# Hybrid decoder trunk on one core: forget-gate tile cleared first, a planner whose operations overlap, and first halves' sums of squares that add two k tiles on VectorE

## The chip, the core and the metric

One core of one Trainium2 chip runs the whole program. The metric is the device time of one execution in microseconds. It is taken as the median of several runs: 1278.13 us for the kernel before, of three runs between 1277.13 and 1283.45. The engines that matter are TensorE (PE, with its weight loads PEld), VectorE (DVE), ScalarE (ACT), GpSimd (POOL) and SyncE (SP), which only issues transfers.

## The reference

Two layers of a decoder trunk work on one sequence of 512 tokens, with 16 learned meta tokens in front (528 rows, width 1024, float32). A layer has a mixer and a feed-forward part (FFN), each between two RMS norms:

```python
h = h + rms_norm(mixer(rms_norm(h, pre_g)), post_g)
h = h + rms_norm(ffn(rms_norm(h, pre_g)), post_g)

def rms_norm(x, g):
    return x * rsqrt(mean(x * x, axis=-1) + 1e-6) * g
```

The mixer makes one projection `w_in` of the normed rows. Its columns are q, k and v of eight attention heads, eight forget-gate logits, a gated convolution of 31 taps and a short one of 3 taps. The attention's logits carry a running sum of the forget gates' logarithms:

```python
log_f = log_sigmoid(f_logit + b_forget)
F = cumsum(log_f, axis=1)
s = q @ k.T * scale + F[:, :, None] - F[:, None, :]    # causal
y_attn = softmax(s) @ v
```

The three groups are normed by head, concatenated and projected by `w_out`. The FFN (inner width 2816) projects up to a gate and a value, passes both through a convolution of 3 taps, and projects `silu(gate) * value` down.

## The kernel before

**Layout.** Activations lie transposed: 128 features in the partitions, 528 rows along the free axis, so the width of 1024 is 8 k tiles (`KD`). Rows are worked in two halves of 264, which the code calls `hf` 0 and 1. Every product in float32 is made from a high and a low part of each operand, `uhi`, `ulo`, `whi`, `wlo`, `yhi`, `ylo`: three matmuls for each product, high by high, high by low and low by high (`mm3`, whose matmuls have L668, and `First.steps`, L709). ACT casts the high part (a weight's at L608, with L2049 for the FFN's up weights and their sums), and DVE takes the low part as the difference. The FFN's up projection combines blocks of weights and of activations so that seven products (L2198) do the work of eight; POOL issues transfers that add weights onto weights for it (`raw<-u`, `u<-raw`, L2086), and their results `s1` to `s4` are split on ACT and DVE as well. A product's result is copied out of PSUM by ACT (`z` at L2211, `yp` at L2373).

**Who sets the order.** The kernel doesn't issue its work in program order. Class `Flow` is a planner: `act`, `dve`, `gp` and `flow.op` hand in operations with an engine, an estimated duration, what they wait for and a priority, and generators hand in stretches of matmuls. `Flow.run` keeps a clock for each engine (`self.free`) and one for TensorE (`self.pe`), always takes what can start first, and moves that engine's clock by the estimated duration. The order in which it takes operations is the order in which they stand in each engine's queue. An engine works its queue strictly in order: where one operation waits, all behind it wait. Where the plan has TensorE idle for longer than `flow.least` (2.0 us, in the mixer 0.7), `Flow.run` puts in idle matmuls of a constant, the fillers (L1775, 128x128).

**Norms.** The sum of squares over the 1024 features of a half goes through class `Norms`. For each pair of k tiles ACT squares 128 x 2 x 264 values (L749; at times DVE does), and DVE adds them onto `acc`, a tile with two slices, one for each k tile of the pair (L765). The last pairs can stay apart as tiles `c` of their own (`n_apart`). `factor` then sums over the partitions: for each of these parts, two matmuls with the constant `om_d` (L792), one for each slice, all into one PSUM tile. These are plain float32. From that ACT and DVE work out the factor (L805 to L812) with which the half is scaled. A norm has a key: ("y", hf) is the norm behind a sub-layer, ("h", hf) the one ahead of the next.

**The mixer's start.** Convolution taps run on DVE (L937, L987, L989). At the same time POOL clears tiles for the attention: parts of `vhi`, `vlo`, `vals`, of `k` and `q` tiles and of `dm` (L439 is the helper `mset`), then `fx` (L1151). `fx` takes the forget-gate logits: `v_proj` makes v in five blocks of rows (L1204), and for each block ACT copies `vhi`, DVE makes `vlo` (L1181) and DVE adds the bias to the eight logit columns into `fx` (L1184). The PSUM bank is free again after these. `forget_gate` then takes logarithm and running sum: DVE prepares `fpre` (L1239), TensorE sums (L1244), DVE copies to `gt` (L1245), TensorE transposes (L1253).

**The attention.** Its matmuls are the logits (L1361, L1405), products of probabilities `ph`, `pl` and v (L1462), and column terms from `dm` (L1385). The remaining projection matmuls (L668) and the convolution's work are planned in between.

## Time and profile before

| | |
|---|---|
| median of three runs | 1278.13 us (1277.13 to 1283.45) |
| the profiled execution | 1277.56 us |
| its span | 1275.8 us |
| mean granted clock of TensorE | 0.995 |
| TensorE busy | 1239.5 us, 97% |
| VectorE busy | 967.7 us, 76% |
| ScalarE busy | 775.6 us, 61% |
| GpSimd busy | 236.2 us, 19% |
| fillers, records of L1775 | 58 |
| VectorE's wait for fx, both layers | 13.1 us |

The span runs from the first to the last instruction that the profiler saw; the execution's own time is 1.8 us longer. A row of the timeline gives the start, the busy time, the engine, the line, the operation, its output and inputs, their shape and how many were put together; in brackets stands the idle time ahead of it and what ended it. A row of the chain of waits gives start, length and the piece of work. A row of a group gives busy time and mean nanoseconds of one. A window's row gives its bounds and length, then for PE, PEld, DVE, ACT and POOL the busy time and the number of instructions, then the clock granted, the DMA share and GB/s. The plain float32 matmuls of `om_d` are recorded twice each.

### The profile page before, as it was taken

The page shows a single profiled execution, that of the slowest core. Times are in us where ns is not written, and L with a number is a line of the kernel's source. Part 1 is how long each engine was busy: PE and PEld are TensorE (multiplying, and loading weights), DVE is VectorE, ACT ScalarE, POOL GpSimd, SP SyncE. Part 2 cuts the span into 40 slices and gives each one's busy share as a digit, 9 for nine tenths or more (in the row PEclk, how much of TensorE's full clock was granted, in tenths as well). Part 3 has the DMA queues.
Part 4 walks back from the last instruction along what each step waited for, and adds up shares of the span by engine and source line. Part 5 has one row for each costly group of instructions (what it writes and reads, how often), then busy time and mean ns, then how long its engine had stood idle before and what let it go on. Part 6 is the DMA issues. An engine that isn't in the chain of part 4 may idle for free.

```text
span 1275.8 us, 24511 instructions
## 1 busy us (share of the span) xinstructions
PE 1239.5 (97%) x9468; PEld 1188.3 (93%) x9468; DVE 967.7 (76%) x1752; ACT 775.6 (61%) x1571; POOL 236.2 (19%) x415
## 2 busy tenths in 40 slices
PE   9999999999999999999999999999998999999996
PEld 8988988999999999999999899889997999999986
DVE  7598877588866777788676988766887587778865
ACT  7256668667755555556672666785676565556552
POOL 1314320002122222120003233200022122122200
PEclk9999999999999999999999999999999999999998
DMA  7131131636486866776340322216386677768641
GB/s 225 51 102 52 47 113 34 206 119 167 102 195 139 188 156 154 172 161 183 115 140 18 111 76 68 60 58 213 131 175 136 155 160 169 163 148 185 144 141 66
DMA packets 73942, 165.85 MB, mean 130 GB/s; under 512 B 8081, under 2 KB 26641, under 8 KB 73313
## 3 DMA queue, kind: packets, MB, share of 16 engines
q1 hardware_dynamic: 52048, 124.86, 30.6%
q0 software_dynamic: 21360, 39.02, 19.0%
q8 instruction: 74, 1.21, 0.4%
q10 hardware_dynamic: 416, 0.40, 0.1%
q14 instruction: 44, 0.35, 0.1%
HBM read 129.14 MB, written 8.65 MB: 108 GB/s over the span
## 4 chain that ended last, share of the span: by engine, by line
PE 79%; DVE 8%; ACT 4%; issue 4%; DMA 2%; POOL 2%; DVEq 0%; ACTq 0%; POOLq 0%
PE psum L668 37%; PE psum L2198 25%; PE psum L709 6%; PE psum L1462 2%; PE psum L1204 2%; PE psum L792 2%; PE psum L1405 1%; DVE cacc L937 1%; DMA c<-acc 1%; DMA raw<-in_w_dram 1%; PE psum L1361 1%; POOL q L439 1%; DMA raw<-u 1%; POOL k L439 1%; PE psum L1532 1%
## 5 line engine op out<-in xcount | busy, mean ns | idle before, releaser
L668 PE MATMUL psum<-yhi,whi 128*128 128x264 f32 (+3 forms) x660 | 187.9, 299 | 3.6 <-ACT yp L2373 2.1
L668 PE MATMUL psum<-ylo,whi 128*128 128x264 f32 (+3 forms) x660 | 184.7, 295 | 1.1 <-DVE ylo L2175 0.8
L668 PE MATMUL psum<-yhi,wlo 128*128 128x264 f32 (+3 forms) x660 | 184.3, 294 | 0.2 <-DVE wlo L612 0.2
L668 PE MATMUL psum<-uhi,whi 128*128 128x264 f32 (+1 forms) x640 | 165.2, 291 | 1.2 <-DVE q L1292 1.2
L668 PE MATMUL psum<-ulo,whi 128*128 128x264 f32 (+1 forms) x640 | 161.0, 284 | 0.5 <-DVE ulo L1947 0.5
L668 PE MATMUL psum<-uhi,wlo 128*128 128x264 f32 (+1 forms) x640 | 160.7, 284 | 0.0
L2124 DVE SCALAR_TENSOR_TENSOR c<-z,pv,c 128x528 f32<-128x528 f32 (+1 forms) x156 | 117.1, 757 | 29.0 <-ACT c L2122 26.4
L612 DVE TENSOR_TENSOR wlo<-raw,whi 128x1024 fp32r<-128x1024 f32 (+2 forms) x84 | 100.5, 1205 | 38.1 <-ACT whi L608 37.1
L668 PEld LDWEIGHTS psum<-yhi,whi 128*128 128x128 f32 x660 | 120.3, 188 | 9.1 <-ACT yp L2373 2.5
L668 PEld LDWEIGHTS psum<-ylo,whi 128*128 128x128 f32 x660 | 120.4, 188 | 4.4 <-DVE ylo L1088 1.1
L668 PEld LDWEIGHTS psum<-yhi,wlo 128*128 128x128 f32 x660 | 120.4, 189 | 3.2 <-DVE wlo L612 0.6
L668 PEld LDWEIGHTS psum<-uhi,whi 128*128 128x128 f32 x640 | 111.9, 188 | 4.4 <-issue 2.4
L2211 ACT COPY z<-psum 128x264 f32<-128x264 f32 (+2 forms) x128 | 48.2, 377 | 107.2 <-PE psum L2198 106.5
L668 PEld LDWEIGHTS psum<-ulo,whi 128*128 128x128 f32 x640 | 112.2, 188 | 0.9 <-DVE ulo L1947 0.7
L668 PEld LDWEIGHTS psum<-uhi,wlo 128*128 128x128 f32 x640 | 112.1, 188 | 0.4 <-DVE wlo L612 0.4
L608 ACT CAST whi<-raw 128x1024 fp32r<-128x1024 f32 (+2 forms) x84 | 85.8, 1034 | 38.7 <-DMA raw<-in_w_dram 20.4
L937 DVE SCALAR_TENSOR_TENSOR cacc<-apad,pv,cacc 128x528 f32<-128x528 f32 x120 | 88.6, 766 | 0.3
L709 PE MATMUL psum<-uhi,whi 128*128 128x264 f32 (+1 forms) x320 | 85.0, 289 | 1.3 <-ACT uhi L840 1.3
L709 PE MATMUL psum<-uhi,wlo 128*128 128x264 f32 (+1 forms) x320 | 83.4, 283 | 0.0
L2052 DVE TENSOR_TENSOR wlo<-raw,whi 128x1024 fp32r<-128x1024 f32 (+4 forms) x78 | 76.4, 980 | 8.6 <-ACT whi L2049 8.2
L2049 ACT CAST whi<-raw 128x1024 fp32r<-128x1024 f32 (+4 forms) x78 | 66.3, 855 | 15.5 <-PE psum L668 10.3
L2198 PE MATMUL psum<-uhi,whi 128*128 128x264 f32 (+1 forms) x256 | 72.8, 284 | 2.2 <-ACT yp L2373 2.2
(317 smaller groups left out, 3732.4 us busy)
## 6 DMA issues: line engine op xcount, KB each, us to landing
raw<-in_w_dram SPq DMA_DIRECT2D x110, 512.0 KB
u<-in_w_dram SPq DMA_DIRECT2D x32, 512.0 KB
u<-in_w_dram POOLq DMA_DIRECT2D x32, 256.0 KB, 5.3
raw<-in_w_dram POOLq DMA_DIRECT2D x32, 256.0 KB, 4.1
u<-raw POOLq DMA_DIRECT2D x32, 256.0 KB, 4.0
raw<-u POOLq DMA_DIRECT2D x32, 256.0 KB, 4.2
raw<-in_w_dram SPq DMA_DIRECT2D x16, 448.0 KB
h_mid<-h SPq DMA_DIRECT2D x4, 1056.0 KB
```

The source lines that it names most:

```text
L439: nc.gpsimd.memset(t.bitcast(F32), val)
L608: nc.scalar.copy(box["hi"][:, :sz], box["raw"][:, :sz])
L612: nc.vector.tensor_sub(lo[:, :sz], box["raw"][:, :sz], box["hi"][:, :sz].bitcast(F32))
L668: nc.tensor.matmul(d, lhsT=w[a][:, k, cols], rhs=rhs(b, k, hf), start=start and i == 0 and p == 0, stop=stop and i == n - 1 and p == 2)
L709: nc.tensor.matmul(self.ps[hf, i], lhsT=self.ws[i].w[a][:, k, :], rhs=self.rhs(b, k, hf), start=k + a + b == 0, stop=k == KD - 1 and b == 1)
L792: nc.tensor.matmul(ps, lhsT=om_d, rhs=box["c"][:, i, :], start=j + i == 0, stop=j + 1 == n_parts and i == 1)
L937: nc.vector.scalar_tensor_tensor(conv[j], in0=src, in1=conv[j], scalar=col("a_dw_w", CK * j + i), op0=ALU.mult, op1=ALU.add)
L2049: nc.scalar.copy(box[name][0], raw())
L2052: return a, dve(dve_us(n), lambda: nc.vector.tensor_sub(box[name][1], raw(), box[name][0].bitcast(F32)), a, prio=prio)
L2124: nc.vector.scalar_tensor_tensor(c, in0=z[:, i:i + n], scalar=wtap(i, t), in1=c, op0=ALU.mult, op1=ALU.add)
L2198: nc.tensor.matmul(d, lhsT=w[i][:, P * k:P * (k + 1)], rhs=terms[b][j][k](), start=start and k + p == 0, stop=k == KH - 1 and p == 2, skip ...
L2211: done[f, name] = act(us, lambda: nc.scalar.copy(z_of(f, e)[:, zin[h]], d[:, lo:]), *after, prio=0)
```

## The change

Three things change. The first is the place at which `fx` is made and cleared: it is now the first tile of the attention's pool, ahead of `vhi`, and its memset is the first of POOL's block.

The second is in the planner. An operation on DVE now gives its engine free 0.08 us before the estimated end, one on ACT 0.095 us before it; when its result is there is counted as before. No instruction is added or taken away by that, but the order of all engines is planned anew.

The third is in the norms. For keys in `norms.folds`, once `acc` is complete, DVE adds its second slice onto its first (128 x 264), and TensorE makes one matmul with `om_d` on the first slice where it made two. That is so for one norm at the opening (("h", 1)), for ("y", 0) and ("h", 0) behind each mixer and behind the first layer's FFN, and for ("y", 0) behind the last FFN: eight in all. VectorE has eight operations more. TensorE has eight matmuls with `om_d` fewer in the norms and 14 fillers fewer (29 to 15). `HOP_US` and `ADD_LAT` only give numbers a name.

```diff
--- before.py
+++ after.py
@@ -56,6 +56,10 @@
 WE = 0.5
 YS = (9, 9)
 NWARM = 10
+PFOLD = 0
+FOLD = ((("h", 1),), (("y", 0), ("h", 0)), (("y", 0), ("h", 0)))
+HOP_US = 0.06
+OVER = {"dve": 0.08, "act": 0.095}
 K1 = 2
 SQD = (2, 6)
 FILLED = 0.8
@@ -69,7 +73,8 @@
 FILL_US = 0.225
 OH = {(0, 0): -3, (0, 4): -2.9, (0, 6): -2.8, **{(1, k): -0.4 for k in range(0, KD, 2)}}
 OW = (-0.46, -0.459)
-ADD_US, ADD_LAT = 1.2, 3.6
+ADD_US = 1.2
+ADD_LAT = 3.6
 PT = ((0.8035, 0.8055), (0.8035, 0.8055))
 D0 = ((0, 0, 0, 0, 5, 10, 15, 20), (0, 0, 0, 0, 5, 10, 15, 20))
 
@@ -249,7 +254,7 @@
 
 
 
-    HOP = 0.06
+    HOP = HOP_US
 
     def __init__(self):
         self.pe = 0.0
@@ -337,7 +342,7 @@
                 for r, slot in takes:
                     r.take(slot)
                 fn()
-                self.free[eng] = start + us
+                self.free[eng] = start + us - OVER.get(eng, 0.0)
                 tok.time = start + us + lat
                 continue
             if self.rings and start > self.pe:
@@ -720,7 +725,7 @@
 
 
         def __init__(self, pool, rs, nc=4, **apart):
-            self.pool, self.nc = pool, nc
+            self.pool, self.nc, self.folds = pool, nc, ()
             self.c, self.acc = Ring(nc), Ring(2)
             self.factors(rs, **apart)
 
@@ -768,6 +773,12 @@
             if k == 0 or k >= KD - 2 * apart:
                 s["parts"][max(0, k // 2 - KD // 2 + apart + 1) if k else 0] = box, slot
                 box["at"] = [a]
+            if k == KD - 2 * apart - 2 and key in self.folds:
+                def fold():
+                    t = s["acc"]["c"]
+                    nc.vector.tensor_add(t[:, 0, :], t[:, 0, :], t[:, 1, :])
+
+                s["at"] = dve(dve_us(n), fold, s["at"], prio=prio + PFOLD)
             if k == KD - 2 * apart - 2:
                 s["acc"]["at"], s["acc"]["there"] = [s["at"]], True
             return a
@@ -788,9 +799,10 @@
                     ps = psum[:, p_slot.buf, :n]
                 s = self.sums[key]
                 box, slot = s["parts"][j]
-                for i in range(2):
-                    nc.tensor.matmul(ps, lhsT=om_d, rhs=box["c"][:, i, :], start=j + i == 0, stop=j + 1 == n_parts and i == 1)
-                tok = flow.mm(2 * 0.0017 * n)
+                m = 1 if j == 0 and key in self.folds else 2
+                for i in range(m):
+                    nc.tensor.matmul(ps, lhsT=om_d, rhs=box["c"][:, i, :], start=j + i == 0, stop=j + 1 == n_parts and i + 1 == m)
+                tok = flow.mm(m * 0.0017 * n)
                 slot.close(tok)
             s["free"] = mine = Slot()
             us, vs = act_us(n), dve_us(n)
@@ -1110,6 +1122,8 @@
         sc_done = {}
 
 
+        fx = T(ap, [P, 5, HEADS], F32, "fx")
+        nc.gpsimd.memset(fx, 0.0)
         vhi = T(ap, [P, 5, WHOLE, VW], F32R, "vhi")
         vlo = T(ap, [P, 5, WHOLE, VW], F32R, "vlo")
         pw_place[0] = lambda: T(ap, [P, 5, WHOLE, VW], F32R, "vlo").rearrange("p b h d -> p (b h d)")
@@ -1147,8 +1161,6 @@
             dm = T(ap, [P, L], F32R, f"dm{j}")
             mset(dm[:, :N_META], 0.0)
             dms.append(dm)
-        fx = T(ap, [P, 5, HEADS], F32, "fx")
-        nc.gpsimd.memset(fx, 0.0)
         gt = T(ap, [P, 5, HEADS], F32, "gt")
         g_hl = [T(mp, [P, L], F32, "sq", 2)[:HEADS].bitcast(F32R) for _ in range(2)]
 
@@ -1793,6 +1805,7 @@
         plan_w(after_mixer[0])
         norms = Norms(sp, [T(sp, [P, L], F32, f"rs{i}", 1) for i in range(NRS)], NCS, h=APS)
         norms.apart["h", 0] = KD // 2 - 1
+        norms.folds = FOLD[0]
         hg, hg_at = T(sp, [P, KD, L], F32, "hg", 1), {}
         for hf in range(2):
             for k in range(0, KD, 2):
@@ -1861,6 +1874,7 @@
             first = First(u_in, iws, {})
             rs = T(fp, [P, L], F32, "rs", 1)
             norms = Norms(fp, [rs])
+            norms.folds = FOLD[1]
             plan = ExitStack()
             plan.enter_context(tc.manual_schedule(engines=every))
             flow.yields = YF[l]
@@ -2473,6 +2487,7 @@
                 wpos[0] += 2
                 rs, rz = (T(fp, [P, L], F32, n, 1) for n in ("rs", "rz"))
                 norms.factors([rs, rz], h=APART)
+                norms.folds = FOLD[2]
                 norms.apart["y", 1] = YA[l]
                 norms.acc = Ring(2)
                 flow.yields = YE[l]
```

How the planner's new order stands, at three places. Line numbers of the changed kernel are 5 to 14 higher for the same statement (L668 is L673, L1462 is L1474, L2373 is L2387). A row is a line, an operation, its output and input tiles and its size; the numbers behind the names tell tiles apart and differ from one kernel to the other.

TensorE's queue in the first layer's attention, before. `ph` and `pl` are probabilities, `om_d` by itself is a filler:

```order
L1405 MATMUL psum_67<-q_88_676,k_80_668 128x400
L1361 MATMUL psum_67<-k_81_669,q_89_677 16x16
L1361 MATMUL psum_67<-k_81_669,q_89_677 128x144
L1775 MATMUL psum_67<-om_d_84 128x128 x3
L1462 MATMUL psum_67<-ph_1382,vhi_651 128x400
L1462 MATMUL psum_67<-pl_1396,vhi_651 128x400
L1462 MATMUL psum_67<-ph_1382,vlo_652 128x400
L1361 MATMUL psum_67<-k_81_669,q_89_677 128x272
L1405 MATMUL psum_67<-q_87_675,k_79_667 128x272
L1405 MATMUL psum_67<-q_88_676,k_80_668 128x272
```

And what follows on such a product of probabilities and v in the changed kernel, at the same part of the attention:

```order
L1474 MATMUL psum_67<-ph_1363,vhi_654 128x400
L1474 MATMUL psum_67<-pl_1376,vhi_654 128x400
L1474 MATMUL psum_67<-ph_1363,vlo_655 128x400
L1417 MATMUL psum_67<-q_88_678,k_80_670 128x272
L1417 MATMUL psum_67<-q_89_679,k_81_671 128x272
L673 MATMUL psum_67<-uhi_111,whi_1043 128x264
L673 MATMUL psum_67<-ulo_112,whi_1043 128x264
L673 MATMUL psum_67<-uhi_111,wlo_1059 128x264
L673 MATMUL psum_67<-uhi_111,whi_1043 128x264
L673 MATMUL psum_67<-ulo_112,whi_1043 128x264
L673 MATMUL psum_67<-uhi_111,wlo_1059 128x264
```

The two filler groups of the late attention (three and four matmuls; one of them is in the rows before) are gone in each layer, and only the group of two ahead of these rows is left; projection products (L673) stand between the products of probabilities and the logits.

ScalarE's queue at the start of the second layer's FFN, before. `yp` are the copies out of PSUM, `whi`, `d0hi`, `s2hi`, `s4hi` high parts of weights, the s ones from POOL's adding transfers:

```order
L2049 CAST d0hi_11140<-draw_11092 128x640
L2049 CAST whi_11272<-raw_11105 128x640
L2373 COPY yp_10321<-psum_67 128x512 x2
L1939 CAST acc_11701<-c_11690 128x2x258
L1939 CAST acc_11716<-c_11697 128x2x258
L2049 CAST s2hi_11718<-u_1023_11204 128x512
L2171 CAST yhi_1074_11738<-c_11634 128x512
L2049 CAST s4hi_11744<-raw_11072 128x512
L2373 COPY yp_10321<-psum_67 128x512
```

And after:

```order
L2063 CAST s2hi_11685<-u_1025_11195 128x512
L2387 COPY yp_10304<-psum_67 128x512
L2063 CAST d0hi_11127<-draw_11082 128x640
L2387 COPY yp_10304<-psum_67 128x512
L2185 CAST yhi_1074_11701<-c_11573 128x512
L2063 CAST whi_11276<-raw_11093 128x640
L2063 CAST s4hi_11728<-raw_11060 128x512
L2387 COPY yp_10304<-psum_67 128x512
L2063 CAST d0hi_11127<-draw_11082 128x640
```

The first copy `yp` now stands ahead of `d0hi` and `whi`, the second ahead of `whi`; the third stands behind `s4hi` as before.

ScalarE's queue at the end of the second layer's FFN, where `w_down`'s last blocks are split, before:

```order
L608 CAST whi_14143<-raw_14094 128x896
L2151 ACTIVATE c_14103<-c_14103 128x512
L2154 ACT_TABLE_LOAD
L608 CAST whi_14167<-raw_14105 128x896
L608 CAST whi_14179<-raw_14123 128x896
L2171 CAST yhi_1152_14193<-c_14103 128x512
L608 CAST whi_14223<-raw_14177 128x896
```

And after:

```order
L2136 ACTIVATE c_14101<-z_952_10309,pv_15_108 128x512
L2165 ACTIVATE c_14072<-c_14072 128x512
L2168 ACT_TABLE_LOAD
L613 CAST whi_14135<-raw_14082 128x896
L2185 CAST yhi_1147_14148<-c_14072 128x512
L613 CAST whi_14157<-raw_14095 128x896
L613 CAST whi_14170<-raw_14113 128x896
```

`yhi` stood behind three casts of weights and stands behind one now. On VectorE the matching `ylo` stood behind the low parts of these weights, and stands ahead of two of them now.

## The prediction

> **What bounds the kernel now.** I read the profile in this order: busy times, chain of waits, PE's group with the most idle time, then the timeline at every place where PE waits.
>
> ```profile
> span 1275.8 us, 24511 instructions
> PE 1239.5 (97%) x9468; PEld 1188.3 (93%) x9468; DVE 967.7 (76%) x1752; ACT 775.6 (61%) x1571; POOL 236.2 (19%) x415
> PE 79%; DVE 8%; ACT 4%; issue 4%; DMA 2%; POOL 2%; DVEq 0%; ACTq 0%; POOLq 0%
> L668 PE MATMUL psum<-yhi,whi 128*128 128x264 f32 (+3 forms) x660 | 187.9, 299 | 3.6 <-ACT yp L2373 2.1
> ```
>
> TensorE is busy 97% of the span and holds 79% of the chain. A matmul less is therefore time saved, if it stands in a dense stretch; a change on another engine is worth only the PE waits that it ends. PE idles 36 us in all, in many small pieces, so the planner can gain some, not tens. The profiled execution took 1277.56 us, 1.8 more than its span and 0.57 less than the median of 1278.13; the sum starts from 1277.56. A measurement of this kernel tells about 0.5% (6.4 us) from no change.
>
> One rule for the rows below: PE's listed ends are modelled and overlap the next start. Matmuls of 264 columns are listed at 0.28 but start 0.12 apart, so a listed idle time understates a hole by about 0.16.
>
> **Folds.** Eight norms drop one om_d matmul each and gain one VectorE add.
>
> ```profile
> 656.62 1.78 PE psum L792 x8
> 255.00:276.00 21.00, 21.00 (x166) 20.64 (x164) 17.21 (x30) 12.85 (x26) 0.00 (x0) 1.00 0.21 71
> 884.00:905.00 21.00, 21.00 (x169) 20.70 (x169) 18.14 (x33) 13.23 (x28) 0.00 (x0) 1.00 0.26 76
> L2244 DVE TENSOR_TENSOR z<-z,psum 128x264 f32<-128x264 f32 x16 | 6.8, 428 | 3.9 <-PE psum L2198 3.8
> ```
>
> The profile records an fp32 om_d matmul twice: 8 records in 1.78 us, so a dropped matmul is 2 x 0.222 = 0.44 us. Two folds lie in each of the windows above (after each layer's mixer; columns are length, then PE, PEld, DVE, ACT, POOL busy): PE is full, so 0.44 each is real there. The other four, at the opening and behind the FFNs, I take as alike. The new add is a 128x264 tensor-tensor of about 0.43 us (an estimate from the L2244 row, which has that size but reads PSUM); DVE has 3.8 and 2.9 us spare in those 21 us, which hides two adds each. Should that cover go, PE waits 0.43 for the add and nothing is gained. Sum: 8 x 0.44 = **-3.5**, bounds -3.5 and 0.
>
> **Clearing fx first.** POOL runs its block of memsets in order, and fx came behind all the k and q ones.
>
> ```profile
> 60.04 0.14 POOL L1151 MEMSET fx<- 128x40 f32 x1
> 53.17 0.49 DVE L987 TENSOR_SCALAR sccx<-cxp,pv 128x528 f32<-128x528 f32 x1
> 60.21 0.17 DVE L1184 TENSOR_TENSOR fx<-psum,pv 128x8 f32<-128x8 f32 x1 [6.55 <-POOL fx L1151]
> 60.30 0.28 PE L1204 MATMUL psum<-wlo,uhi 128*128 128x264 f32 x1
> 61.44 0.39 PE L1204 MATMUL psum<-whi,uhi 128*128 128x264 f32 x1 [0.86 <-DVE vlo L1181]
> 61.67 0.28 PE L1204 MATMUL psum<-whi,ulo 128*128 128x264 f32 x1
> 690.52 0.39 PE L1204 MATMUL psum<-whi,uhi 128*128 128x264 f32 x1 [0.30 <-DVE vlo L1181]
> ```
>
> DVE stood at fx for 6.55 us, with vlo queued behind it, and PE needed the bank that vlo frees. The start goes from 60.30 to 61.44 instead of 60.42 (1.02) and the next from 61.44 to 61.67 (0.11 more than usual): 1.13. In layer 2 it is 0.30 + 0.16 + 0.11 = 0.57. Cleared early, fx costs no DVE wait; of the 6.55 us that DVE gets back in this layer, most were never PE's. The memset (0.14 us) moves the rest of POOL's block back by as much as it had stood behind it. Sum **-1.7**, bounds -1.7 and 0.
>
> **The planner.** OVER lets it believe DVE free 0.08 us, and ACT 0.095 us, before each operation ends, so every engine's order is dealt anew. The trace must say whether the belief is true:
>
> ```profile
> 61.98 1.45 DVE L937 SCALAR_TENSOR_TENSOR cacc<-apad,pv,cacc 128x528 f32<-128x528 f32 x2
> L937 DVE SCALAR_TENSOR_TENSOR cacc<-apad,pv,cacc 128x528 f32<-128x528 f32 x120 | 88.6, 766 | 0.3
> 975.10 1.06 ACT L2373 COPY yp<-psum 128x512 f32<-128x512 f32 x2
> 982.87 0.58 ACT L2373 COPY yp<-psum 128x512 f32<-128x512 f32 x1
> 11.70 0.43 DVE L806 SCALAR_TENSOR_TENSOR rs<-psum,rs 128x264 f32<-128x264 f32 x1 [0.29 <-ACT rs L805]
> 12.16 0.43 DVE L812 SCALAR_TENSOR_TENSOR rs<-rs 128x264 f32<-128x264 f32 x1
> ```
>
> Two DVE operations of 0.766 take 1.45, so the second starts 0.08 early; two ACT copies of 0.58 take 1.06, 0.10 early. The belief is true where the second doesn't need the first; where it does (12.16 follows 11.70 by 0.46), there is no overlap. [...]
>
> *Opening.* One pair of L824 (row below) moves ahead of the work that the last ulo waits for. The PE waits there are 0.3 to 0.4 each; the pair's own 0.61 is what the last of them can gain: **-0.6**, bounds -1 and 0.
>
> *Fillers in the mixer.* PE's idle matmuls L1775 go where the plan has a gap of 0.7 us and more.
>
> ```profile
> 17.31 0.61 DVE L824 TENSOR_SCALAR hg<-h,pg 128x264 f32<-128x264 f32 x2
> 20.48 0.39 PE L709 MATMUL psum<-ulo,whi 128*128 128x264 f32 x1 [0.34 <-DVE ulo L841]
> 92.54 0.61 PE L1775 MATMUL psum<-om_d 128*128 128x128 f32 x4
> 109.09 0.88 PE L1775 MATMUL psum<-om_d 128*128 128x128 f32 x6
> 110.20 0.45 PE L1462 MATMUL psum<-ph,vhi 128*128 128x400 f32 x1 [0.24 <-ACT yta L1480]
> 113.09 1.05 PE L1775 MATMUL psum<-om_d 128*128 128x128 f32 x8
> ```
>
> In each layer the groups of 6 and 8 records vanish, and projection products stand in their places, so the time goes to work that was due anyway. A record costs (1.05 - 0.61) / 4 = 0.11; 14 records in two layers: 28 x 0.11 = 3.1. The waits behind them (0.24 and like ones, some 1.3 per layer) may go too or stay. **-3.1**, bounds -5.8 and 0 (a planned gap that closes only on paper).
>
> *Forget gate.*
>
> ```profile
> 78.27 0.41 PE L1244 MATMUL psum<-fpre,ones_r 128*128 128x40 f32 x2 [0.66 <-DVE fpre L1239]
> 80.19 0.71 PE L1253 MATMUL psum<-ident,gt 128*8 128x128 f32 x5 [0.70 <-DVE gt L1245]
> ```
>
> In the new order the first of these stands 12 matmuls (12 x 0.12 = 1.5 us) earlier on PE, the second 18. PE waits there already, and everything on PE queues behind the waiting matmul. The DVE chain ahead of it gets shorter by some 0.4 to 1.1 us, from the count of operations that go behind it. I take **+2** for two layers, bounds 0 and +3.
>
> *Second layer's FFN start.*
>
> ```profile
> 974.68 7.64 DMA raw<-u
> 976.22 0.39 PE L2198 MATMUL psum<-uhi,whi 128*128 128x258 f32 x1 [1.55 <-ACT yp L2373]
> 982.35 0.62 ACT L2049 CAST s4hi<-raw 128x512 fp32r<-128x512 f32 x1 [2.69 <-DMA raw<-u]
> 983.50 0.77 PE L668 MATMUL psum<-yhi,whi 128*128 128x512 f32 x1 [2.09 <-ACT yp L2373]
> 984.00:988.00 4.00, 4.00 (x19) 3.60 (x18) 0.83 (x1) 0.60 (x3) 1.70 (x2) 0.63 0.91 248
> ```
>
> ACT's third yp copy stands behind a cast that waits for a transfer (7.64 us), and PE waits for the copy; then the granted clock is 0.63 for 4 us, another 4 x 0.37 = 1.5. In the new order the first yp copy stands ahead of two casts that it followed, but s4hi is still ahead of the third copy, and whether its transfer is issued earlier I can't tell. The first wait should go: **-1.5**; bounds 0 and -5.1 (1.55 + 2.09 + 1.5).
>
> *The end.*
>
> ```profile
> 1227.21 0.94 ACT L608 CAST whi<-raw 128x896 fp32r<-128x896 f32 x1 [2.01 <-DMA raw<-in_w_dram]
> 1228.06 0.61 ACT L2171 CAST yhi<-c 128x512 fp32r<-128x512 f32 x1
> 1228.72 0.39 PE L668 MATMUL psum<-yhi,whi 128*128 128x256 f32 x1 [1.31 <-ACT yhi L2171]
> 1229.93 0.39 PE L668 MATMUL psum<-ylo,whi 128*128 128x256 f32 x1 [0.82 <-DVE ylo L2175]
> ```
>
> yhi stood behind two weight casts, the second of which waits 2.01 us for a transfer. Now it stands ahead of both, and ylo ahead of their halves on DVE. Both holes go: (1.31 + 0.16) + (0.82 + 0.27) = **-2.6**. The weight cast at 1227.21 is then next to be late, but its first product comes 53 matmuls (6.4 us) behind the yhi one. Bounds -2.6 and 0.
>
> **Sum.** -3.5 - 1.7 - 0.6 - 3.1 + 2 - 1.5 - 2.6 = -11.0. Some 800 other pieces move, mostly where PE is full and nothing is due; each term also supposes that nothing else is late at its place. I give back 2 for that, chosen, not worked out: -9.0, **1268.6 us**.
>
> **Rivals.**
> 1. *The plan gains on paper only.* Folds and fx hold (-5.2), the forget gate costs 2, the closed gaps open elsewhere: 1274.4. A new stall at the first layer's FFN start, where POOL's adding transfers and casts come in a new order, like 983.50's (5.1), would on top of the forecast give 1273.7. For it: PE was already 97% busy, the removed gaps were planned ones. Against: the end and fx are rows, not plans. 0.20.
> 2. *The folds don't shorten.* The add lies between the last square and the norm's first matmul; where PE stands waiting for acc already, the add lengthens it as much as the matmul saved. Then -9.0 + 3.5 gives 1272.1. For it:
>
> ```profile
> 285.36 0.94 PE L792 MATMUL psum<-acc,om_d 128*128 128x264 f32 x3 [0.34 <-DVE acc L765]
> ```
>
> PE does wait for acc there, at a norm without a fold. Against: the two full windows. 0.05.
> 3. *Slower: DVE doesn't overlap in chains.* In the 884 window it has 33 operations: planned 33 x 0.08 = 2.6 us too early, with 2.9 us to spare. If most of them depend on each other, the orders after the four sublayers are made for a DVE that is 2.6 us ahead, and PE waits as much for the norm's result: 1277.6 - 5.2 + 4 x 2.6 = 1282.8, with a clock loss of 1.5 at one of them 1284.3. It decides from 6.5 us of new waits on, where it eats the 5.2 and more. Against: the pair of 1.45 us, and that most neighbours on DVE belong to different tiles. 0.08.
> 4. *The clock.* Without fillers the attention phase has longer idle stretches, and the clock drops as at 984:
>
> ```profile
> 1226.00:1232.00 6.00, 3.79 (x27) 3.18 (x27) 3.16 (x5) 2.13 (x3) 0.00 (x0) 1.00 1.03 369
> ```
>
> Four places at 1.5 give 1274.6. Against: holes of 1.31 and 0.82 in this window left the clock at 1.00, and the longest hole that the removed fillers leave is 0.88 + 0.24 + 0.16 = 1.3. 0.05. The Trainium skill, "TensorE: Matmul & The Clock Gate", "Part 1: The HAM clock gate", puts the drop behind an idle window of about 3.4 us; the drop at 984 came after holes of 1.55 and 2.09, not one of that length, so the rule alone doesn't clear this rival.
>
> **How the numbers follow.** The forecast's case has 0.62, the rivals 0.20, 0.05, 0.08 and 0.05. With the favourable bounds of fillers and FFN start the time is 1268.6 - 2.7 - 3.6 = 1262.3, and with no cost at the gate 1260.3; I cut at 1261, and above at 1277, which takes in rivals 1, 2 and 4. Left out: rival 3 and the far tail, some 0.15. Faster by over 0.5% is below 1271.7: nearly all of the forecast's case and a little of the others, 0.65; within 0.5%: 0.28; slower: 0.07.
>
> **What would show it.** No wait for fx on DVE; L1204's holes gone in both layers; 8 om_d matmuls fewer and no acc wait over 0.4 us in their place; yhi and ylo without holes near 1225; two filler groups less per layer, and PE's idle time in the attention phase not grown; forget-gate waits of 0.66 and 0.70 grown to about 1.2. Wrong would be: new waits over 2 us at an FFN start, or PE waits that grow with every DVE chain.

## The result, and the profile after

| | before | changed |
|---|---|---|
| median | 1278.10 us (18 runs) | 1275.25 us (18 runs) |
| lowest to highest | 1275.21 to 1283.45 | 1274.04 to 1276.57 |
| ratio | 1 | 0.9977, interval 0.9969 to 0.9985 |
| the profiled execution's span | 1275.8 | 1273.6 |
| TensorE busy | 1239.5 | 1236.4 |

The change gained 2.9 us, 0.23%, where 9.5 us against the median were forecast. The busy times and the chain of waits of the changed kernel:

```profile
span 1273.6 us, 24443 instructions
PE 1236.4 (97%) x9424; PEld 1183.0 (93%) x9424; DVE 969.0 (76%) x1760; ACT 768.5 (60%) x1571; POOL 229.7 (18%) x415
PE 69%; DVE 10%; ACT 8%; issue 6%; DMA 5%; POOL 1%; SPq 0%; DVEq 0%; POOLq 0%; ACTq 0%
```

TensorE's busy time fell by 3.1 us and the span by 2.2. By the prediction's amounts the eight matmuls and the 28 filler records should take 6.6 us away, and busy time is no clean measure of work: with fx alone, which has every matmul of before, it falls by 3.9 (to 1235.6). The chain says more: TensorE's share fell from 79% to 69%, and that of VectorE and ScalarE rose from 12% to 18%, so more of the span hung on other engines.

A part of the gain goes with the clock. In 61 executions of the kernel before, timed beside the experiments, the mean granted clock was 0.9952; in the 18 of the changed kernel it was 0.9968. Among those 61 a clock lower by 0.001 went with about 1.0 us more, so some 1.6 of the 2.9 us are the clock's (an estimate).

Where it happened is seen by cutting the span at instructions that every version has, by the start of their rows. This table is worked out from the timelines of TensorE; each number is the length of a stretch in the kernel before, and then how much longer or shorter it is in the others (us). The columns behind the changed one are experiments that are told of below.

| stretch | before | changed | fx alone | folds alone | overlap alone | fx and overlap |
|---|---|---|---|---|---|---|
| start to the first v product | 51.65 | -0.91 | -0.43 | -0.43 | -0.45 | -0.56 |
| first v products | 12.70 | -1.13 | -1.13 | 0.00 | -0.74 | -1.13 |
| mixer, to its norm's first om_d | 191.48 | +1.55 | -1.92 | +0.21 | +6.40 | +1.24 |
| norm, up products, FFN start | 157.50 | +1.48 | +0.11 | +0.60 | +1.69 | +1.44 |
| FFN | 177.38 | +0.77 | -0.02 | -0.01 | +0.07 | +0.28 |
| FFN's end | 31.48 | +0.71 | -0.04 | +0.66 | +0.59 | +0.25 |
| norm, second layer's opening | 59.00 | -0.62 | 0.00 | +0.20 | +0.01 | +0.05 |
| v products | 12.24 | -0.57 | -0.57 | 0.00 | -0.57 | -0.57 |
| mixer | 191.48 | +1.74 | -1.82 | +0.38 | +5.82 | +1.39 |
| norm, up products | 91.31 | +1.26 | +0.04 | +1.58 | +1.06 | +1.60 |
| FFN's start | 66.32 | -3.94 | -2.02 | -2.92 | -3.92 | -3.92 |
| FFN | 173.14 | +0.02 | +0.01 | 0.00 | +0.02 | +0.01 |
| FFN's end | 33.44 | -1.89 | +0.08 | -0.10 | -1.08 | -0.87 |
| last norm | 14.93 | -0.78 | +0.01 | -0.73 | -0.03 | -0.03 |

In the changed kernel both mixers and both stretches behind their norms got longer, 6.0 us in sum, where the prediction had them shorter by 2.9 (two folds each, fillers and gate). The first row is no evidence for the change: versions that differ nowhere near the opening vary there by 0.5 us and more. Of the gain at the second FFN's start, 2 us aren't either: that stretch is shorter by that in every later run, whatever was changed.

The new waits stand in TensorE's timeline of the changed kernel (idle time ahead of the instruction in brackets, and what ended it):

```profile
75.92 0.71 PE L1265 MATMUL psum<-ident,gt 128*8 128x128 f32 x5 [0.69 <-DVE gt L1257]
83.13 0.36 PE L1373 MATMUL psum<-k,q 128*128 128x272 f32 x1 [0.81 <-DVE mcol L1380]
225.89 0.51 PE L673 MATMUL psum<-yhi,whi 128*128 128x264 f32 x2 [0.78 <-ACT yhi L1099]
226.66 0.39 PE L673 MATMUL psum<-ylo,whi 128*128 128x264 f32 x1 [0.26 <-DVE ylo L1100]
228.68 0.39 PE L673 MATMUL psum<-yhi,whi 128*128 128x264 f32 x1 [0.54 <-ACT acc L754]
282.79 0.39 PE L714 MATMUL psum<-uhi,whi 128*128 128x264 f32 x1 [0.69 <-ACT uhi L890]
284.01 0.51 PE L714 MATMUL psum<-ulo,whi 128*128 128x264 f32 x2 [0.47 <-DVE ulo L893]
1229.70 0.39 PE L673 MATMUL psum<-yhi,whi 128*128 128x256 f32 x1 [0.49 <-DVE yp L1672]
```

All but the first are new; for `gt` TensorE waited 0.70 us before as well. At 225 TensorE has nothing left to do but the output projection, and waits for the last head norms; at 282 it waits for the normed rows that the next sub-layer reads. Of the two holes near 1225 one smaller one is left, now for VectorE's addition that frees the PSUM bank.

### The profile page after: what moved, and what is told of

Its sections match the earlier page's. It is cut to its first block, busy times and chain, and to the rows that moved or that the text cites. A ratio compares the mean times of both kernels' runs of the same rounds, so it can differ in the third digit from the quotient of the medians.

```text
span 1273.6 us, 24443 instructions
## 1 busy us (share of the span) xinstructions
PE 1236.4 (97%) x9424; PEld 1183.0 (93%) x9424; DVE 969.0 (76%) x1760; ACT 768.5 (60%) x1571; POOL 229.7 (18%) x415
## 4 chain that ended last, share of the span: by engine, by line
PE 69%; DVE 10%; ACT 8%; issue 6%; DMA 5%; POOL 1%; SPq 0%; DVEq 0%; POOLq 0%; ACTq 0%
PE psum L673 30%; PE psum L2212 24%; PE psum L714 6%; PE psum L1216 4%; DMA c<-acc 3%; PE psum L1474 2%; ACT whi L613 1%; PE psum L804 1%; PE psum L1417 1%; DVE wlo L617 1%; PE psum L1373 1%; DVE cacc L949 1%; DMA raw<-in_w_dram 1%; DVE rs_t L1082 1%; ACT yhi L1099 1%
## 5 line engine op out<-in xcount | busy, mean ns | idle before, releaser
L673 PE MATMUL psum<-yhi,whi 128*128 128x264 f32 (+3 forms) x660 | 186.6, 298 | 3.4 <-ACT yhi L1099 1.8
L673 PE MATMUL psum<-ylo,whi 128*128 128x264 f32 (+3 forms) x660 | 184.1, 294 | 0.7 <-DVE ylo L1100 0.5
L673 PE MATMUL psum<-yhi,wlo 128*128 128x264 f32 (+3 forms) x660 | 183.8, 293 | 0.2
L673 PE MATMUL psum<-uhi,whi 128*128 128x264 f32 (+1 forms) x640 | 164.3, 289 | 0.0
L673 PE MATMUL psum<-ulo,whi 128*128 128x264 f32 (+1 forms) x640 | 161.5, 285 | 2.0 <-DVE ulo L1961 1.7
L673 PE MATMUL psum<-uhi,wlo 128*128 128x264 f32 (+1 forms) x640 | 160.6, 283 | 0.0
L673 PEld LDWEIGHTS psum<-yhi,whi 128*128 128x128 f32 x660 | 120.1, 188 | 7.2 <-ACT yhi L1099 2.2
L673 PEld LDWEIGHTS psum<-ylo,whi 128*128 128x128 f32 x660 | 120.2, 188 | 3.7 <-DVE ylo L1100 0.9
L673 PEld LDWEIGHTS psum<-yhi,wlo 128*128 128x128 f32 x660 | 120.3, 188 | 3.2 <-DVE wlo L617 0.6
L673 PEld LDWEIGHTS psum<-ulo,whi 128*128 128x128 f32 x640 | 112.1, 188 | 3.3 <-DVE ulo L1961 3.2
L673 PEld LDWEIGHTS psum<-uhi,whi 128*128 128x128 f32 x640 | 112.0, 188 | 1.8 <-issue 1.6
L673 PEld LDWEIGHTS psum<-uhi,wlo 128*128 128x128 f32 x640 | 112.2, 189 | 0.0
```

What stands on the lines that cost most here:

```text
L673: nc.tensor.matmul(d, lhsT=w[a][:, k, cols], rhs=rhs(b, k, hf), start=start and i == 0 and p == 0, stop=stop and i == n - 1 and p == 2)
```

## The experiments

All start from the changed kernel, with parts taken back. Each was timed against the kernel before on the same chip; the ratio is given with its 95% interval.

**Each part alone.**

```diff
-OVER = {"dve": 0.08, "act": 0.095}
+OVER = {}
-FOLD = ((("h", 1),), (("y", 0), ("h", 0)), (("y", 0), ("h", 0)))
+FOLD = ((), (), ())
```

Both edits leave fx first alone; the folds alone and the overlap alone have the other edit instead, and `fx` made and cleared at its old place.

> The kernel before with fx made and cleared first, nothing else. Both theories: the wait of DVE for fx goes in both layers, the stretch of the first v products gets 1.1 us shorter in the first layer and 0.6 in the second, all other stretches keep their length within 0.2; about -1.7 us.

> The kernel before with the eight folds alone, planned with the old clocks. Theory A (the folds save their matmuls, the new order by the overlap numbers gave it back): about -3.5 us, and the stretch from the norm behind a mixer to the FFN's first seven products is 0.9 us shorter in each layer. Theory B (behind the norm it is the chain through ACT and DVE to the first uhi and ulo that TensorE waits for, so a dropped matmul turns into a wait): between -1 and 0 us, with new waits of TensorE for uhi and ulo of 0.3 to 0.7 us behind the norm.

> The kernel before with the overlap numbers alone. Theory A: slower by 2 to 4 us in sum, with the stretches of the mixers 1.6 us longer and those behind the mixers' norms over 1 us longer each, against 4 us won at the second FFN's start and 2 at the end. Theory B: the stretches behind the norms keep their length, and the sum is -2 to 0 us.

> The changed kernel without the overlap numbers (fx first and folds). Theory A: -5 us, faster than the changed kernel by 2 us. Theory B: -2 to -3 us, about the changed kernel's time.

| | median us | ratio |
|---|---|---|
| fx alone | 1269.85 | 0.9947 (0.9934 to 0.9961) |
| folds alone | 1277.14 | 1.0007 (0.9997 to 1.0017) |
| overlap alone | 1286.19 | 1.0074 (1.0058 to 1.0090) |
| fx and folds | 1271.28 | 0.9964 (0.9951 to 0.9977) |

Clearing fx first is alone worth 0.53% (6.7 us), more than the whole change, and the other two parts take more than half of it back. Both theories of its expectation had 1.7 us. The v products did gain that; the mixers got 1.9 and 1.8 us shorter as well, with the same order of work (TensorE's, ScalarE's and VectorE's queues hold the same operations in the same places as before). Fx and folds came to 5.2 us less than before, theory A's number, by luck: fx brings 6.7 of it, and the folds take 1.4 back. The overlap alone, 9.7 us slower, missed both theories. With fx alone, the forget gate's rows on TensorE are these, with no idle time ahead of either (before: 0.66 and 0.70):

```profile
75.56 0.39 PE L1256 MATMUL psum<-fpre,ones_r 128*128 128x40 f32 x2
76.73 0.71 PE L1265 MATMUL psum<-ident,gt 128*8 128x128 f32 x5
```

and on VectorE the last piece of fx, then the last operation on `fpre` and the copy to `gt`, of before and of fx alone (rows between them left out):

```profile
71.01 0.15 DVE L1184 TENSOR_TENSOR fx<-vsum,pv 16x8 f32<-16x8 f32 x1
...
78.05 0.16 DVE L1239 TENSOR_TENSOR fpre<-fpre,fe 128x8 f32<-128x8 f32 x1
79.93 0.20 DVE L1245 COPY gt<-psum 128x40 f32<-128x40 f32 x1
```

```profile
66.47 0.15 DVE L1196 TENSOR_TENSOR fx<-vsum,pv 16x8 f32<-16x8 f32 x1
...
74.60 0.16 DVE L1251 TENSOR_TENSOR fpre<-fpre,fe 128x8 f32<-128x8 f32 x1
76.48 0.20 DVE L1257 COPY gt<-psum 128x40 f32<-128x40 f32 x1
```

TensorE came to the last v product 1.6 us earlier, VectorE to the end of `fpre` 3.45 us earlier. Before, VectorE still carried a part of its 6.55 us of standing when the forget gate began, and TensorE paid for it a second time: (0.66 + 0.70) + 2 x (0.16 + 0.11) = 1.90 us by the overlap and restart amounts of the prediction, against the 1.92 measured.

The overlap alone meets the late fx with an order that was made for an early VectorE: TensorE's forget-gate matmul waits 2.94 us for `fpre`, and a product 0.93 for `vlo`. Right behind that the granted clock is 0.50 for 6.83 us, which makes up to 3.4 of the 6.40 us that the first mixer lost.

```profile
66.49 0.39 PE L673 MATMUL psum<-uhi,whi 128*128 128x264 f32 x1 [0.93 <-DVE vlo L1193]
78.57 0.41 PE L1256 MATMUL psum<-fpre,ones_r 128*128 128x40 f32 x2 [2.94 <-DVE fpre L1251]
79.71:86.54 6.83, 6.39 (x30) 5.44 (x29) 5.99 (x12) 1.52 (x5) 0.00 (x0) 0.50 0.27 78
```

The folds alone gain nothing: theory B of their expectation in kind, with its wait for ulo (0.67 us). The window between the norm's factor and the last ulo behind the first mixer shows VectorE's part, before and then with folds alone (after the length: PE, PEld, DVE, ACT and POOL busy):

```profile
271.80:286.00 14.20, 13.86 (x109) 13.45 (x108) 13.93 (x29) 8.24 (x19) 0.00 (x0) 1.00 0.38 154
```

```profile
271.00:286.00 15.00, 14.33 (x118) 14.06 (x117) 14.93 (x31) 8.34 (x18) 0.00 (x0) 1.00 0.36 145
```

VectorE is busy 13.93 of 14.20 us there, so an operation more on it has no cover. But the operation also changes the plan. With fx alone, in the order of before, four operations `z` stand behind the last ulo in VectorE's queue:

```profile
280.39 0.48 DVE L893 SCALAR_TENSOR_TENSOR ulo<-h,pg,uhi 128x264 fp32r<-128x264 f32 x1
281.75 1.45 DVE L1865 TENSOR_TENSOR z<-psum,rz 128x264 f32<-128x264 f32 x4
```

With folds alone they stand ahead of it, and the plan gives TensorE 14 filler records as well, behind which it still waits for that ulo:

```profile
281.86 1.72 PE L1787 MATMUL psum<-om_d 128*128 128x128 f32 x14
283.57 1.45 DVE L1865 TENSOR_TENSOR z<-psum,rz 128x264 f32<-128x264 f32 x4
284.92 0.49 DVE L893 SCALAR_TENSOR_TENSOR ulo<-h,pg,uhi 128x264 fp32r<-128x264 f32 x1
285.47 0.51 PE L714 MATMUL psum<-ulo,whi 128*128 128x264 f32 x2 [0.67 <-DVE ulo L893]
```

The order of z and ulo goes with the loss in nearly all versions. In the second layer, whose stretch "norm, up products" ends ahead of the FFN's start, the ten versions with z first are 0.8 to 1.8 us longer than before. Of the seven with z last, five lie between -0.6 and +0.3, and the two with the overlap on one engine at +0.6 and +1.2. The versions with both overlap numbers have z first without any fold, so there the folds find that price paid already: the changed kernel (0.9977) is faster than fx and overlap without folds (1.0006, below). No run puts z back alone, so this cause is read from the queues and not tested.

**The overlap with fx first, whole and by halves.**

```diff
-FOLD = ((("h", 1),), (("y", 0), ("h", 0)), (("y", 0), ("h", 0)))
+FOLD = ((), (), ())
-OVER = {"dve": 0.08, "act": 0.095}
+OVER = {"dve": 0.08}
```

(All four start from the changed kernel without folds. The first run has the first edit alone, the third `{"act": 0.095}`; the fourth empties `OVER` at the opening and ahead of each mixer and fills it behind.)

> The changed kernel without folds (fx first and the overlap numbers). Theory A2 (the overlap costs by itself, in the mixers, whatever fx does): the stretch from the first v products to the mixer's norm is about 191 us per layer and more, as in the changed kernel (192.7), against 189.4 with fx alone; time about 1274 to 1276 us. Theory B2 (the overlap cost 9.7 us without fx only because it met the late fx; with fx early it is harmless, and the folds make the changed kernel slower than fx alone): mixers at 189.5 us, time about 1268 us.

> fx first, overlap on VectorE alone (0.08). If the loss in the mixers comes from VectorE's clock, the mixers take 192 us and the time is 1273 to 1276 us; if from ScalarE's, it stays at fx alone's 1270 us.

> fx first, overlap on ScalarE alone (0.095). If the loss in the mixers comes from ScalarE's clock, the mixers take 192 us and the time is 1273 to 1276 us; if from VectorE's, it stays at fx alone's 1270 us.

> fx first, overlap numbers from the norm behind each mixer to the end of that layer's FFN only; opening and mixers planned with the old clocks. If the overlap loses in the mixers and wins at the FFN's start and end: the mixers stay at fx alone's 189.4 us, the two holes of 1.4 and 0.8 us at the last yhi and ylo go, and the time is 1265 to 1268 us, under fx alone. If the overlap loses behind the norms as well: 1270 us or more.

| | median us | ratio |
|---|---|---|
| fx and overlap | 1277.21 | 1.0006 (0.9996 to 1.0017) |
| fx, overlap on VectorE | 1295.12 | 1.0140 (1.0126 to 1.0154) |
| fx, overlap on ScalarE | 1290.47 | 1.0107 (1.0093 to 1.0121) |
| fx, overlap in the FFNs | 1270.21 | 0.9943 (0.9931 to 0.9955) |

Theory A2 held in kind: beside fx alone the overlap costs 3.2 us in each mixer (+1.24 against -1.92), and 7 us in all (7.4 by the medians). My two expectations on the halves were wrong: neither half is harmless, and each alone is far worse than both (25 and 21 us over fx alone). The loss isn't that of one engine's wrong number; the order itself comes out better or worse with each set of numbers. A part of the two halves' loss is the clock: ahead of their last norm TensorE ran 10.2 us (VectorE's half) and 17.1 us (ScalarE's) at a granted clock of 0.50, the changed kernel none. At half speed that is up to 5 and 8.5 us. In the FFNs the overlap gains at the ends (-3.8 at the second start, -1.4 at the second end) what it loses behind the norms (+2.4 and +0.9, all against before), and ends level with fx alone.

**The folds by place.** All four have fx first and an empty `OVER`.

```diff
+FOLD = ((), (("h", 0),), (("h", 0),))
```

```diff
+FOLD = ((), (("y", 0),), (("y", 0),))
```

For the third run, with the h folds, the matmul is kept and the operation does nothing useful; for the fourth, with all eight folds, GpSimd adds:

```diff
-                    nc.vector.tensor_add(t[:, 0, :], t[:, 0, :], t[:, 1, :])
+                    nc.vector.tensor_max(t[:, 0, :], t[:, 0, :], t[:, 0, :])
-                m = 1 if j == 0 and key in self.folds else 2
+                m = 2
```

```diff
-                    nc.vector.tensor_add(t[:, 0, :], t[:, 0, :], t[:, 1, :])
+                    nc.gpsimd.tensor_add(t[:, 0, :], t[:, 0, :], t[:, 1, :])
-                s["at"] = dve(dve_us(n), fold, s["at"], prio=prio + PFOLD)
+                s["at"] = gp(0.8, fold, s["at"], prio=prio + PFOLD)
```

> fx first, old clocks, and only the three folds of the norm ahead of the next sub-layer (h, first half). If VectorE is the bound between the norm behind a sub-layer and the last ulo (it has no idle time from 268 to 283 us in the run with fx alone), an add there delays uhi and ulo: the stretch from the mixer's norm to the FFN's first seven products gets longer by 0.4 to 1.5 us in each layer, and the time is 1 to 3 us over fx alone. If TensorE is the bound there: 0.44 us less at each of three places, 1.3 us under fx alone.

> fx first, old clocks, and only the four folds of the norm behind a sub-layer (y, first half). There VectorE has idle time, so the dropped matmuls should count: 0.4 us less at each place, 1.5 us under fx alone. If the add delays the norm's factor, which everything behind it needs: 0 to 2 us over fx alone.

> As the one with the three h folds, but TensorE keeps both matmuls, and the operation on VectorE takes the maximum of the first slice with itself, which changes nothing: the cost of the VectorE operation alone. If VectorE's extra operation is what costs, the stretches behind the norms are as long as with the h folds or 0.4 us longer; if it is hidden, they are as with fx alone.

> fx first, old clocks, all eight folds, with the add on GpSimd, which has no work behind the norms. If VectorE's time is what the folds cost, the stretches behind the norms get 0.4 us shorter per fold than with fx alone: 1 to 3 us under fx alone, about 1267 us. If it is the length of the chain to the factor, GpSimd's slower add (I take about 1 us) makes it as slow as the folds on VectorE or slower: 1271 to 1275 us.

| | median us | ratio | norm behind mixer 1 | mixer 2 | FFN 1 end and norm |
|---|---|---|---|---|---|
| fx alone | 1269.85 | 0.9947 (0.9934 to 0.9961) | +0.11 | +0.04 | -0.04 |
| with h folds | 1271.59 | 0.9958 (0.9944 to 0.9972) | +1.15 | +1.77 | +0.24 |
| VectorE's operation alone | 1272.75 | 0.9967 (0.9954 to 0.9980) | +0.56 | +1.84 | +1.80 |
| with y folds | 1269.98 | 0.9945 (0.9933 to 0.9958) | -0.92 | +0.82 | +0.62 |
| all folds on GpSimd | 1275.26 | 0.9992 (0.9982 to 1.0002) | +2.26 | -0.61 | +6.29 |

(The three columns on the right are stretches of the table above, in us against the kernel before; the last adds two rows.) The h folds make the stretches behind the mixers' norms 1.0 and 1.7 us longer than with fx alone. VectorE's operation alone, with both matmuls kept, does so by 0.5 and 1.8: the operation in the plan is what costs, and the dropped matmul is no gain where TensorE then waits for ulo. The y folds gain 1.0 behind the first mixer, lose 0.8 behind the second and come out level. The queues go with this: z stands ahead of the last ulo, with 14 filler records on TensorE, behind both mixers with the h folds and with VectorE's operation alone, and behind the second alone with the y folds. On GpSimd the add takes 0.72 to 2.91 us:

```profile
251.68 0.74 POOL L779 TENSOR_TENSOR acc<-acc 128x264 f32<-128x264 f32 x1 [27.24 <-DVE acc L770]
905.87 2.91 POOL L779 TENSOR_TENSOR acc<-acc 128x250 f32<-128x250 f32 x1 [17.60 <-DVE acc L770]
```

With it the stretch behind the second mixer is 0.61 us shorter, and z stands last there. At the end of the first FFN and behind its norm 6.3 us are lost. Most of that is fillers, with one more wait for uhi behind them:

```profile
640.81 6.41 PE L1787 MATMUL psum<-om_d 128*128 128x128 f32 x56
648.18 0.39 PE L714 MATMUL psum<-uhi,whi 128*128 128x264 f32 x1 [0.95 <-ACT uhi L852]
```

With fx alone no filler stands there. Why the plan has uhi so late with the add on GpSimd stays open.

**The chain of head norms.**

```diff
-            c = act(us, lambda: nc.scalar.activation(box["t"], box["r"], AF.Square), b, prio=prio)
+            full = eps != RMS_EPS
+            c = act(us, lambda: full and nc.scalar.activation(box["t"], box["r"], AF.Square), b, prio=prio)
...
```

The two VectorE operations behind it have the same `full and`, and the scaling reads `box["r"]` in their place: in both runs the refining of the factor is left out for the head norms of the convolution groups.

> The changed kernel with a shorter chain in the head norms of the two convolution groups: the squaring on ScalarE and the two VectorE operations that refine the factor are left out (one ScalarE and two VectorE operations less for each of 8 halves a layer), planned as before. If that chain is what TensorE waits for at the first w_out products (0.78, 0.26 and 0.54 us in the changed kernel), these waits go and each mixer gets 2 to 3 us shorter; time about 1270 us. If not, less than 0.5 us per mixer.

> The same shortening (the same operations of the convolution groups' head norms left out) with fx first alone. TensorE does not wait there with fx alone, so whichever theory holds the mixers keep their length within 0.5 us; time 1269 to 1270 us.

The changed kernel came to 1272.56 us (0.9963, 0.9949 to 0.9977), fx alone to 1269.41 (0.9939, 0.9927 to 0.9952). In the changed kernel each mixer got 1.66 and 1.67 us shorter, with fx alone 0.38 and 0.59. The waits for yhi and ylo at 225.89 and 226.66 are gone; that for acc is left:

```profile
227.33 0.39 PE L673 MATMUL psum<-yhi,whi 128*128 128x264 f32 x1 [0.48 <-ACT acc L754]
```

So the chain of head norms was a bound at the changed mixers' end, and hardly one with fx alone; what was left out of it accounts for about 1.2 of the 3.5 us that a mixer of the changed kernel has over fx alone (1.7 less the 0.4 to 0.6 that the shortening is worth anyway). The expected 2 to 3 us were too much. ScalarE's rows in the changed kernel show how the chain lost its pace:

```profile
217.52 0.41 ACT L1099 CAST yhi<-sccx 128x264 fp32r<-128x264 f32 x1 [0.94 <-DVE sccx L1096]
221.48 0.41 ACT L1099 CAST yhi<-cacc 128x264 fp32r<-128x264 f32 x1 [0.94 <-DVE cacc L1096]
225.43 0.41 ACT L1099 CAST yhi<-cacc 128x264 fp32r<-128x264 f32 x1 [0.94 <-DVE cacc L1096]
```

Two halves go through it side by side, so both are on VectorE at the same time, and ScalarE stands 0.94 us each time. With fx alone these casts stand in between other norms' steps, and ScalarE waits 0.11 us for one and 1.31 us for the last.

**Putting the good parts together.**

```diff
+            norms.folds = () if l else (("y", 0),)
+                norms.folds = (("y", 0),) if l else ()
```

The first run has these two lines for the folds behind the mixers and behind the FFNs, the opening's fold as in the change, and an empty `OVER`; the second fills `OVER` from the start of each FFN's seven products on and empties it ahead of the next mixer.

> fx first, old clocks, with the three folds whose stretches got shorter so far: opening, first layer's mixer norm, last norm. If gains of single stretches add up: 0.4 + 0.9 + 0.7, that is 2 us under fx alone, about 1268 us. If the plan behind a fold changes enough to lose it elsewhere: 1269 to 1271 us.

> The same three folds and fx first, with the overlap numbers on only from the start of each FFN's seven products to that FFN's end. If the second FFN's start and end gain as in the changed kernel (2 us over fx alone at the start, 1 to 2 at the end) and nothing else moves: 1264 to 1267 us. If not: 1268 us or more.

They took 1270.63 us (0.9950, 0.9937 to 0.9962) and 1271.52 (0.9959, 0.9946 to 0.9971), so the gains of single stretches didn't add up. The folded norms behind the first mixer and at the very end kept theirs in the first run (-0.91 and -0.75 against before). The first FFN's end lost 0.9, and in both runs the second FFN's end is 1.68 us longer than before, where fx alone is 0.08 longer. In both the granted clock falls to 0.50 for 3.41 us there, which costs up to 1.7; in the second run, with the overlap on, behind one wait of 2.53 us where fx alone has 1.40 and 0.83:

```profile
1223.98 0.39 PE L673 MATMUL psum<-yhi,whi 128*128 128x256 f32 x1 [2.53 <-DVE yp L1672]
1224.84:1228.25 3.41, 3.41 (x18) 3.41 (x18) 1.64 (x2) 3.41 (x7) 0.00 (x0) 0.50 0.29 112
```

The best version is the plainest: fx first and nothing else, 1269.85 us, under both kernels (the interval of its ratio lies below that of the changed kernel). With the y folds, or with the overlap in the FFNs, it is level.

## Why the prediction was right or wrong

The sign was right and the time lies in the range; the size was three times too large. Three terms failed: what fx holds up was put at a third of its worth, the fillers' time didn't come back, and the folds' cover wasn't there. The errors partly cancelled. What came nearest was the first rival, the plan that gains on paper only (1274.4), and that by luck: it has the folds holding and the gate costing 2; of its mechanism only the gaps that open elsewhere were seen, in the mixers. By the steps of the sum, changed kernel against before in one profiled execution each:

- **fx, -1.7.** Right for what it counted (1.13 and 0.57, as worked out), but the term was mis-sized: fx alone is worth 1.13 + 1.92 + 0.57 + 1.82 = 5.4 us. The step that failed is "of the 6.55 us that DVE gets back in this layer, most were never PE's". The forget gate's waits were quoted in the prediction itself, as work of the planner's; they were the second half of the wait for fx.
- **Forget gate, +2.** Wrong in sign. Both waits went with fx; the new order, which puts these matmuls earlier, brought 0.69 of the second back in each layer, and 0.23 of the first in the first layer.
- **Fillers, -3.1.** The fillers went (58 records to 30), and the time didn't. "The time goes to work that was due anyway" is where it failed: the attention's last product starts 9.4 us earlier than before (205.09 against 214.53), and what is left, the output projection, then waits for the head norms. Against fx alone the overlap makes each mixer 3.2 us longer. In the first mixer the three waits at 225.89 to 228.68 come to 1.6, of which the shortened chain of head norms shows about 1.2, and the waits across the attention grow by 0.4 (83.13 above is the largest). With the 1.4 us of the fillers that went, some 2.6 us are left. They stand in matmuls that start farther apart with no wait listed, and weren't taken apart.
- **Folds, -3.5.** The step that failed is the cover: "DVE has 3.8 and 2.9 us spare in those 21 us, which hides two adds each". Most of the spare time lay ahead of the second half's factor, in holes of 2.16 and 1.50 us; from that factor to the last ulo VectorE is busy 13.93 of 14.20 us. The add cost 0.43 us, as estimated, but it also turned the order of z and ulo. What the eight folds brought beside fx is +1.4 us (1271.28 against 1269.85), not -3.5. Beside the overlap, which has that order anyway, they brought -2.0 by the medians (1275.25 against 1277.21, on two chips; by the ratios 0.9977 against 1.0006), but behind the mixers' norms only 0.0 and -0.3 of the 0.9 each that was counted on. Only the last norm's held its gain everywhere, 0.73 to 0.78 us in each version that has it on VectorE.
- **Second FFN's start, -1.5.** Measured -3.94, in the bounds, by luck. The first wait, which was to go, stayed at 1.28 us (1.55 before); the second one went, which was left open. Half of the gain isn't the change's: with fx alone, where the order is that of before, the stretch has -2.02, and with the folds -2.92; the overlap brings the rest. The clock of 0.63 was 0.50 for 3.41 us, up to 1.7 us. Whether other executions of the kernel before have that drop isn't shown. With fx alone, with a hole of 1.58 us in the same place, the clock stayed:

```profile
977.23 0.50 PE L673 MATMUL psum<-yhi,whi 128*128 128x512 f32 x1 [1.58 <-ACT yp L2387]
977.50:981.50 4.00, 4.00 (x24) 3.52 (x24) 1.52 (x2) 1.20 (x3) 1.60 (x2) 1.00 0.88 243
```

- **The end, -2.6.** Measured -1.89, by the mechanism that was forecast: both holes went, and one of 0.49 came, for a PSUM bank.
- **Opening, -0.6.** Measured -0.91, which holds the opening's fold too; too small beside the 0.5 us by which it varies.
- **The 2 us given back** were too few. The slower rival's mechanism (VectorE late in chains) was near: with the overlap on one engine only, this kernel is slower than before by 14 to 18 us, a part of it by the clock. Rival 4, the clock, came the other way round in the changed kernel, which lost less to it than the kernel before (mean clock 0.997 against 0.995).

## What to carry to other kernels

Where an engine stands for long, follow its backlog to every later wait for it, not to the first one: two thirds of what fx cost (3.7 of 5.4 us) were paid some 17 us on. Spare time of an engine counts only between an added operation and the one that needs it; measure that stretch, not the stage around it, and look whether the planner deals a new order around the operation. A scheduler's numbers that are truer one by one need not give a better order, and an order that closes gaps in the plan can use up the work that would have covered a chain at the end: time the parts of a change apart, since a good one can hide two that cost.

## What was not expected of the hardware

A hole of 2.09 us on TensorE, 5 us behind one of 1.55, was followed by half the clock; a hole of 1.58 at the same place was not, and with fx and overlap one of 1.86 us at 1230.79 was not either. What tells them apart is how much idle time falls into one piece of a fixed division of time. In all 18 profiles the stretches at one granted clock, between the first change of the clock and the last, take whole multiples of 3.41 us. Cut into pieces of 3.41 us by these changes, the kernel before has TensorE busy 1.32 us of one piece, and the next is at 0.50:

```profile
980.16:983.57 3.41, 1.32 (x7) 0.76 (x5) 1.95 (x4) 1.22 (x3) 0.00 (x0) 1.00 0.94 191
983.57:986.98 3.41, 3.41 (x13) 3.12 (x14) 0.95 (x2) 0.51 (x1) 1.45 (x2) 0.50 0.80 219
```

The hole of 1.86 us is cut in two by such a border, and neither piece is idle for more than 1.4 us:

```profile
1230.79 0.39 PE L673 MATMUL psum<-yhi,whi 128*128 128x256 f32 x1 [1.86 <-DVE yp L1672]
1226.90:1230.31 3.41, 2.03 (x17) 1.82 (x16) 1.43 (x3) 0.94 (x1) 0.00 (x0) 1.00 0.98 353
1230.31:1233.72 3.41, 2.93 (x24) 2.93 (x25) 2.11 (x3) 2.95 (x6) 0.00 (x0) 1.00 0.50 163
```

Over all profiles, every piece at the full clock with 1.83 us of idle time or more was followed by one at 0.50 (29 of 29, the end of each kernel among them). With less, up to 1.72 us, the clock stayed, but for three pieces with 1.26 to 1.43 us in the runs with the overlap on one engine. The Trainium skill, "TensorE: Matmul & The Clock Gate", "Part 1: The HAM clock gate", puts the drop behind an idle window of about 3.4 us; here a piece of that length that was idle for little more than half had it.

The folds' add (128 by 264, in the second layer also by 250 and 256) took 0.43 us on VectorE, and 0.72 to 2.91 us on GpSimd. Four of GpSimd's eight stood where VectorE was idle and took 0.72 to 0.75 us; beside the others, which took 0.76, 0.80, 1.71 and 2.91, VectorE worked. The 2.91 stood where VectorE was busy nearly throughout (from 903 to 909 us, 5.43 of 6.00):

```profile
903.00:909.00 6.00, 5.89 (x51) 5.69 (x50) 5.43 (x12) 3.12 (x8) 2.91 (x1) 1.00 0.01 3
```

VectorE paid as well: its making of ulo beside that add took 0.91 us, where 0.48 is usual. The Trainium skill, "GPSIMD Engine Reference", "1. Specifications", has GpSimd share its interfaces to SBUF with VectorE, with contention when VectorE's instruction has two inputs there; these rows agree, but no run tells which of VectorE's operations hold GpSimd up.
